# Stick-breaking attention: part of the weight multiplies on GpSimd, with the second sigmoid written to SBUF

## The chip, the cores and the metric

The kernel runs on one core of one Trainium2 chip. The metric is the device time of one execution in microseconds (us), as the median of several runs of the same program. A profile of one execution is used beside it; its span goes from the first to the last instruction.

## The reference

One layer of a transformer block on x of shape (1, 2048, 1024): two kinds of attention side by side, an output projection, and a SwiGLU feed-forward network. The change lies in the stick-breaking attention, which has 8 heads of 64 columns:

```python
def stick_breaking_attention(q, k, v):
    # A[t,s] = beta_ts * prod_{s<j<t}(1 - beta_tj), s < t
    z = einsum('bqhd,bkhd->bhqk', q, k) * 64 ** -0.5
    log_1mb = where(s < t, log_sigmoid(-z), 0.0)
    rem = cumsum(log_1mb, axis=keys, reverse=True) - log_1mb
    a = where(s < t, exp(log_sigmoid(z) + rem), 0.0)
    return einsum('bhqk,bkhd->bqhd', a, v)
```

So for a query t each key s gets beta = sigmoid(z), times the product of (1 - beta) = sigmoid(-z) over all keys between s and t. The other half of the width is differential attention (4 heads, softmax). The outputs of both are normed, joined, multiplied by w_out and added to x; the feed-forward network follows.

## The kernel before

**Stages.** The program has eight head groups. Groups 0 to 3 are differential attention, groups 4 to 7 stick-breaking, two heads each. For each group `proj` multiplies the normed input with 384 columns of w_in (16 row tiles, L320), splits the result into two float16 parts (`split_psum`, L327 or L329 for the high part and L330 for the low one), and transposes q and k by DMA. The projection of the next group is emitted between the attention units of this one (`advance`), and in the last group the output projection (L761) is emitted in its place. The feed-forward network comes behind and holds the second half of the span.

**A unit of stick-breaking.** `stage_a(i, m, b)` takes 128 queries (row tile i), one head m and a block b of up to 1024 keys, in chunks c of up to 512 keys, the last chunk first. There are 192 units with 320 chunks, 224 of them full. For each chunk:

- TensorE writes the scores into a PSUM tile `sc` (L448; four such buffers).
- ScalarE writes sigmoid(-z) into the SBUF tile `om` (L554) and then sigmoid(z) over the scores in `sc` (L555).
- VectorE scans `om` from its end to its start, which leaves the running product in it (L557). The instruction names `sc` as its second operand, which the operation `bypass` doesn't use.
- VectorE multiplies beta from `sc` with the scan shifted by one key, into the SBUF tile `be` (L558). It is the last to read `sc`.

After the chunks, `split_t` splits `be` into two float16 parts in a buffer `s16` (three of them): ScalarE casts the high part (L89), GpSimd subtracts it for the low part (L98). A DMA transpose on SP's queue (L403) brings both into a tile `aT` (five). `stage_b` multiplies `aT` with the values on TensorE (L458), up to five units behind `stage_a`. `be` and `om` come from one pool of nine tiles `z4`; the profile shows both as z.

**What sets the order.** Each engine works off its instructions in order. A scheduler of the framework sets that order when the program is built; it times the instructions by its own model. Which engine gets a piece of work is settled earlier, in the Python code. `note(e, ns)` books planned time to ScalarE, VectorE or GpSimd. `pick(...)` gives the next piece to the engine whose booked load plus cost is least, and books it. `level()` sets all loads to zero, at every fourth row tile of a head group. `split_psum` and `tt` use `pick` too, so what is booked at one place changes the choice at others. Before the change, a chunk booked 3.15 w + 350 to VectorE, w being its keys, and its multiply had no choice.

Of the kernel before, what the change touches and what calls it, by code (L numbers as in the profile page):

```python
# [15 lines left out]
AF = mybir.ActivationFunctionType  # L16
ALU = mybir.AluOpType
# [4 lines left out]
S, D, P = 2048, 1024, 128  # L22
# [37 lines left out]
def block(tc, a, out):  # L60
    nc = tc.nc
    PE, ACT, DVE, POOL, SP = nc.tensor, nc.scalar, nc.vector, nc.gpsimd, nc.sync
    top = ExitStack()
    with top:
# [8 lines left out]
        def note(e, ns):  # L73
            load[e] += ns * KW[e]

        def pick(**cost):
            e = min(cost, key=lambda k: load[k] + cost[k] * KW[k])
            load[e] += cost[e] * KW[e]
            return e

        def level():
            for k in load:
                load[k] = 0.0
# [16 lines left out]
        def pri(k):  # L100
            def deco(f):
                @functools.wraps(f)
                def g(*args):
                    with tc.high_priority(PRI[k]) if PRI[k] else nullcontext():
                        return f(*args)
                return g
            return deco

        def nm(s):
            uid[0] += 1  # L110
            return f"{s}{uid[0]}"
# [139 lines left out]
        with ExitStack() as ph1:  # L251
# [6 lines left out]
            def z4():  # L258
                return zp.tile([P, 1028], F32, tag="z4", bufs=ZB, name=nm("z4"))
# [137 lines left out]
            @pri("spl")  # L397
            def split_t(src, n, he="ADP", le="DP"):
                s16 = s16p.tile([P, 2048], F16, tag="s16", bufs=SB, name=nm("s16"))
                to16(s16[:, :n], src, n, he)  # L400
                tt(s16[:, n : 2 * n], src, s16[:, :n], ALU.subtract, n, le)
                aT = sp.tile([P, 16, P], F16, tag="aT", bufs=AB, name=nm("aT"))
                SP.dma_start_transpose(aT[:, : 2 * n // P, :], s16[:, : 2 * n])  # L403
                return aT
# [36 lines left out]
            def fq(g, i):  # L441
                k = 2 if g == NG - 1 else 4
                return (i % k, k)

            @pri("sc")
            def score_chunk(G, sc, i, q, m, w, cut=False):
                for o in range(2):
                    PE.matmul(sc[:, : 128 * w].rearrange("p (t n) -> p t n", n=P), lhsT=G["q"][i // 4][:, 2 - 2 * o + m, i % 4, :], rhs=G["k"][q][:, m, 0:w, :], start=o == 0, stop=o == 1)  # L448
                if cut:
                    PE.matmul(sc[:, 128 * w - P : 128 * w], lhsT=idb[:], rhs=tri[:], start=False, stop=True, skip_group_check=True)  # L450

            @pri("pv")
            def pv(G, yp, y0, aT, b, n, o, wd, start, stop):
                nb = n // P
                for j in range(nb):
                    v = G["v"][2 * b + j // 4][:, j % 4, :]
                    for q, (a_, v_) in enumerate(((j, o), (j, o + wd), (nb + j, o))):
                        PE.matmul(yp[:, y0 : y0 + wd], lhsT=aT[:, a_, :], rhs=v[:, v_ : v_ + wd], start=start and j == 0 and q == 0, stop=stop and j == nb - 1 and q == 2, skip_group_check=True)  # L458
# [77 lines left out]
            def sb_attn(g, G):  # L536
                last = {}

                @pri("at")
                def stage_a(i, m, b):  # L540
                    L = (i + 1) * 128
                    n = min(1024, L - 1024 * b)
                    be, om = z4(), z4()
                    if b == i // 8:
                        DVE.memset(om[:, n : n + 1], 8192.0)
                    else:
                        DVE.tensor_copy(om[:, n : n + 1], last[m][:, 0:1])
                    last[m] = om
                    for c in range((n - 1) // 512, -1, -1):
                        lo, hi = 512 * c, min(512 * c + 512, n)  # L550
                        w = hi - lo
                        sc = ps.tile([P, 512], F32, tag="sc", bufs=4, name=nm("sc"))
                        score_chunk(G, sc, i, 2 * b + c, m, w // P, b == i // 8 and hi == n)
                        ACT.activation(om[:, lo:hi], sc[:, :w], AF.Sigmoid, scale=G["nkz"][:])  # L554
                        ACT.activation(sc[:, :w], sc[:, :w], AF.Sigmoid, scale=G["kz"][:])  # L555
                        ov = om[:, lo:hi][:, ::-1]
                        DVE.tensor_tensor_scan(ov, ov, sc[:, :w], om[:, hi : hi + 1], op0=ALU.mult, op1=ALU.bypass)  # L557
                        DVE.tensor_tensor(be[:, lo:hi], sc[:, :w], om[:, lo + 1 : hi + 1], ALU.mult)  # L558
                        note("A", 1.7 * w + 400)
                        note("D", 3.15 * w + 350)  # L560
                    return n, split_t(be[:, :n], n, "A", "P")

                ypd = {}

                def stage_b(i, m, b, n, aT):
                    r, k = fq(g, i)
                    if i // k not in ypd:
                        ypd[i // k] = ps.tile([P, 512], F32, tag="yp", name=nm("yp"))
                    yp = ypd[i // k]
                    pv(G, yp, P * r + 64 * m, aT, b, n, 128 * m, 64, r == 0 and m == 0 and b == i // 8, r == k - 1 and m == 1 and b == 0)  # L570
                    if m == 1 and b == 0 and r == k - 1:
                        finish(g, G, i, k, yp)
                        G["fin"] = i + 1

                pend = []
                done = 0
                for i in range(NT):
                    if i % 4 == 0:
                        level()
                    for b in range(i // 8, -1, -1):  # L580
                        for m in range(2):
                            n, aT = stage_a(i, m, b)
                            pend.append((i, m, b, n, aT))
                            if len(pend) > PD:
                                stage_b(*pend.pop(0))
                            done += n // P + CS
                            yield done / (272 + 48 * CS), (i + 1 if b == 0 and m == 1 else i)
                for u in pend:
                    stage_b(*u)
# [638 lines left out]
```

## Time and profile before

| | us |
|---|---|
| median of 3 runs (lowest to highest) | 2779.86 (2775.68 to 2783.71) |
| span of the profiled execution | 2785.0 |

The profiled execution lies just above the highest of the three runs, within their scatter. Busy time by stage:

| us from the start | stage | PE | VectorE | ScalarE | GpSimd | granted clock |
|---|---|---|---|---|---|---|
| 0 to 616 | projections, differential attention | 541.54 | 506.08 | 356.88 | 393.19 | 0.96 |
| 616 to 1405 | stick-breaking, with projections and then the output projection | 642.97 | 664.99 | 581.59 | 419.79 | 0.94 |
| 1405 to 2100 | rest of the output projection, feed-forward network with its weights' preparation | 631.76 | 504.91 | 301.48 | 410.69 | 0.97 |
| 2100 to 2785 | feed-forward network, second half | 673.61 | 324.86 | 121.81 | 221.56 | 1.00 |

A row's busy time is to be held against the length of its stretch, 616, 789, 695 and 685 us. In three of the four stages PE is the busiest engine; in stick-breaking it is VectorE. PE is TensorE's matmuls, PEld its weight loads, DVE is VectorE, ACT ScalarE, POOL GpSimd, SP the queue that issues the DMAs. An arrow in a row of waits points to who was waited for. L-numbers are lines of the kernel before.

### The profile page before, as it was taken

What the parts mean: (1) busy time and instruction counts of PE and PEld (TensorE: products, weight loads), DVE (VectorE), ACT (ScalarE), POOL (GpSimd) and SP (SyncE); (2) the same over time, 40 slices, a digit from 0 to 9 for tenths busy, and PEclk for the clock granted to TensorE, in tenths of its full rate; (3) what the DMA queues carried; (4) which work ended last, traced back from release to release, by engine and by line L of the source; (5) the groups of instructions that cost most, each with busy time, mean ns of one, the idle gap of its engine ahead of it and who ended that gap; (6) DMA issues with size and microseconds to landing.
All of it is one profiled execution on the core that took longest, in us unless ns stands there. A gap on an engine that the chain in (4) does not pass through costs nothing. (4 is left out here: it accounts for less than half of the span.)

```text
span 2785.0 us, 45469 instructions
## 1 busy us (share of the span) xinstructions
PE 2489.9 (89%) x17084; PEld 1409.0 (51%) x17084; DVE 2000.8 (72%) x3782; ACT 1361.8 (49%) x2543; POOL 1445.2 (52%) x1008
## 2 busy tenths in 40 slices
PE   6998989888878786888889798989999999999998
PEld 4665556555545453557775343444444444444443
DVE  6888879687989989876756877777786644434445
ACT  4665656466878788765644534443442212111121
POOL 2567767665544555546665656565654332322323
PEclk9999999999999897999999999999999999999999
DMA  6788787789999998997796565655658844635534
GB/s 225 199 167 184 147 188 163 164 174 205 198 205 198 192 182 160 190 198 205 197 309 253 184 235 189 221 187 191 240 170 299 327 155 178 227 125 190 211 129 166
DMA packets 649133, 551.91 MB, mean 198 GB/s; under 512 B 506624, under 2 KB 574208, under 8 KB 638672
## 3 DMA queue, kind: packets, MB, share of 16 engines
q1 hardware_dynamic: 647088, 546.92, 71.2%
q8 instruction: 134, 2.20, 0.3%
q0 software_dynamic: 512, 1.36, 0.2%
q10 hardware_dynamic: 1312, 0.72, 0.1%
q14 instruction: 87, 0.71, 0.1%
HBM read 265.27 MB, written 151.52 MB: 150 GB/s over the span
## 5 line engine op out<-in xcount | busy, mean ns | idle before, releaser
L98 POOL TENSOR_TENSOR s<-z,s 128x1024 f16<-128x1024 f32 (+7 forms) x288 | 474.1, 1654 | 334.8 <-ACT s L89 299.3
L320 PE MATMUL pj<-w,xt 128*128 128x384 f16 x3072 | 572.3, 334 | 32.6 <-DVE st L330 11.6
L320 PEld LDWEIGHTS <-xt 128*128 128x128 f16 x3072 | 299.9, 100 | 241.8 <-issue 36.3
L448 PE MATMUL sc<-kT,qT 128*128 128x512 f16 (+3 forms) x1280 | 346.9, 362 | 74.6 <-DVE z L558 34.4
L1034 PE MATMUL pd<-wd,act 128*128 128x512 f16 x1848 | 406.2, 379 | 3.3 <-DVE hs L1040 2.4
L557 DVE TENSOR_TENSOR_SCAN z<-z,sc 128x512 f32<-128x512 f32 (+3 forms) x320 | 355.5, 1112 | 68.6 <-ACT sc L555 65.1
L458 PE MATMUL yp<-v,aT 128*128 128x64 f16 (+1 forms) x4896 | 281.2, 207 | 80.0 <-DMA aT<-s 79.2
L458 PEld LDWEIGHTS <-aT 128*128 128x128 f16 x4896 | 245.2, 102 | 169.4 <-DMA aT<-s 105.1
L936 PEld LDWEIGHTS <-wg 128*128 128x128 f16 x1848 | 183.9, 100 | 264.3 <-issue 58.8
L98 POOL TENSOR_TENSOR hs<-hs,cu 128x512 f32<-128x512 f32 x132 | 170.5, 1297 | 238.2 <-DVE cu L1040 82.6
L936 PEld LDWEIGHTS <-wu 128*128 128x128 f16 x1848 | 181.0, 98 | 222.1 <-issue 9.0
L1034 PEld LDWEIGHTS <-act 128*128 128x128 f16 x1848 | 180.6, 98 | 222.6 <-issue 4.7
L98 POOL TENSOR_TENSOR act<-cg,act 128x512 f16<-128x512 f32 x117 | 160.8, 1385 | 247.7 <-ACT act L992 141.5
L98 POOL TENSOR_TENSOR fst<-fst 128x512 f32<-128x512 f32 x97 | 179.6, 1852 | 167.6 <-DVE wd L215 78.6
L1040 DVE SCALAR_TENSOR_TENSOR hs<-pd,c,hs 128x512 f32<-128x512 f32 x192 | 142.1, 748 | 160.8 <-PE pd L1034 159.1
L89 ACT CAST s<-z 128x384 f16<-128x384 f32 (+7 forms) x216 | 170.1, 788 | 151.5 <-DMA aT<-s 56.4
L554 ACT ACTIVATE z<-sc,c 128x512 f32<-128x512 f32 (+3 forms) x320 | 202.6, 633 | 10.6 <-PE sc L448 6.5
L558 DVE TENSOR_TENSOR z<-sc,z 128x512 f32<-128x512 f32 (+3 forms) x320 | 193.3, 606 | 8.1
L992 ACT CAST act<-cg 128x512 f16<-128x512 f32 x132 | 80.6, 617 | 234.2 <-DVE cg L998 190.9
L555 ACT ACTIVATE sc<-sc,c 128x512 f32<-128x512 f32 (+3 forms) x320 | 194.8, 609 | 0.0
L761 PE MATMUL po<-wo,mt 128*128 128x256 f16 x1536 | 181.3, 276 | 11.0 <-DVE xf L764 6.3
L936 PE MATMUL pm<-X,wg 128*128 128x512 f16 x792 | 179.1, 379 | 1.2 <-ACT bx L1109 1.2
(233 smaller groups left out, 4028.4 us busy)
## 6 DMA issues: line engine op xcount, KB each, us to landing
xt<-xs SPq DMA_DIRECT2D x112, 512.0 KB, 4.4
hs<-hd SPq DMA_DIRECT2D x96, 512.0 KB, 4.3
hd<-hs SPq DMA_DIRECT2D x80, 512.0 KB, 3.2
split<-wg SPq DMA_DIRECT2D x11, 1792.0 KB, 10.5
split<-wu SPq DMA_DIRECT2D x11, 1792.0 KB, 10.3
split<-wd SPq DMA_DIRECT2D x11, 1792.0 KB, 10.4
wg<-split SPq DMA_DIRECT2D x11, 1792.0 KB, 7.3
wd<-split SPq DMA_DIRECT2D x11, 1792.0 KB, 8.4
```

The lines of the kernel that those rows point to most:

```text
L89: ACT.copy(dst, src)
L98: (DVE if e == "D" else POOL).tensor_tensor(dst, a_, b_, op)
L320: PE.matmul(pj[:, :384], lhsT=xv[:, xi, kt, :], rhs=G["w"][:, wi, kt, :], start=n == 0, stop=n == 23)
L448: PE.matmul(sc[:, : 128 * w].rearrange("p (t n) -> p t n", n=P), lhsT=G["q"][i // 4][:, 2 - 2 * o + m, i % 4, :], rhs=G["k"][q][:, m, 0:w, ...
L458: PE.matmul(yp[:, y0 : y0 + wd], lhsT=aT[:, a_, :], rhs=v[:, v_ : v_ + wd], start=start and j == 0 and q == 0, stop=stop and j == nb - 1 a ...
L554: ACT.activation(om[:, lo:hi], sc[:, :w], AF.Sigmoid, scale=G["nkz"][:])
L555: ACT.activation(sc[:, :w], sc[:, :w], AF.Sigmoid, scale=G["kz"][:])
L557: DVE.tensor_tensor_scan(ov, ov, sc[:, :w], om[:, hi : hi + 1], op0=ALU.mult, op1=ALU.bypass)
L558: DVE.tensor_tensor(be[:, lo:hi], sc[:, :w], om[:, lo + 1 : hi + 1], ALU.mult)
L761: PE.matmul(po[:, sl], lhsT=mt[:, kt, P * xi : P * xi + P], rhs=wos[2 * h + n][wi][:, kt, :], start=q == 0, stop=q == 23)
L936: PE.matmul(ps_[:].rearrange("p (t n) -> p t n", n=P), lhsT=wv[:, wo, wi, 128 * kt : 128 * kt + 128], rhs=X[xo][:, :, xi, kt, :], start=st ...
L1034: PE.matmul(po[:], lhsT=act[:, ao, xi, 128 * j : 128 * j + 128], rhs=W["d"][:, wo, wi, :], start=start and u == 0 and q == 0, stop=u == nu ...
```

## The change

For each chunk, `pick` now chooses between VectorE ("D") and GpSimd ("P") for the multiply. On "D" all is as before. On "P" the second sigmoid is written to `be` in SBUF and not to `sc`, and GpSimd multiplies `be` in place with the shifted scan. The fixed booking to VectorE falls to the scan's share.

```diff
-                        ACT.activation(sc[:, :w], sc[:, :w], AF.Sigmoid, scale=G["kz"][:])
+                        e = pick(D=1.04 * w + 155, P=2.4 * w + 100)
+                        beta = sc[:, :w] if e == "D" else be[:, lo:hi]
+                        ACT.activation(beta, sc[:, :w], AF.Sigmoid, scale=G["kz"][:])
                         ov = om[:, lo:hi][:, ::-1]
                         DVE.tensor_tensor_scan(ov, ov, sc[:, :w], om[:, hi : hi + 1], op0=ALU.mult, op1=ALU.bypass)
-                        DVE.tensor_tensor(be[:, lo:hi], sc[:, :w], om[:, lo + 1 : hi + 1], ALU.mult)
+                        (DVE if e == "D" else POOL).tensor_tensor(be[:, lo:hi], beta, om[:, lo + 1 : hi + 1], ALU.mult)
                         note("A", 1.7 * w + 400)
-                        note("D", 3.15 * w + 350)
+                        note("D", 2.08 * w + 200)
```

In the built program 148 of the 320 multiplies stand on GpSimd: 117 of the 224 with 512 keys, and 6, 16 and 9 of the 32 each with 384, 256 and 128. Of the 80 units with 1024 keys, 50 have one chunk on each of the two engines. Other choices move with the bookings. Of the projection copies of stick-breaking groups, 45 of `v` and 19 of `st` go from ScalarE (L327) to VectorE (L329). After the output projection 6 subtractions of 1024 elements and 11 of 512 go from GpSimd to VectorE.

The rows below are the built order at one place in the third stick-breaking group, where full units follow each other. Lines of the changed kernel are two higher behind the diff: the second sigmoid is L557, the scan L559, the multiply L560. The scan is printed as SCALAR_TENSOR_TENSOR. z42533 is `be` and z42534 `om` of one unit, z42539 and z42540 of the next, z42547 and z42548 of the one behind; sc2541 and sc2542 are the two chunks of the second. VectorE before:

```order
L557 SCALAR_TENSOR_TENSOR z42534_14931<-z42534_14931,sc2536_14940 128x512
L558 TENSOR_TENSOR z42533_14930<-sc2536_14940,z42534_14931 128x512
L557 SCALAR_TENSOR_TENSOR z42540_14971<-z42540_14971,sc2541_14973 128x512
L558 TENSOR_TENSOR z42539_14970<-sc2541_14973,z42540_14971 128x512
L545 MEMSET z42548_15048 128x1
L557 SCALAR_TENSOR_TENSOR z42540_14971<-z42540_14971,sc2542_14980 128x512
L558 TENSOR_TENSOR z42539_14970<-sc2542_14980,z42540_14971 128x512
```

VectorE with the change, the same units:

```order
L560 TENSOR_TENSOR z42533_14930<-sc2535_14933,z42534_14931 128x512
L547 COPY z42540_14971<-z42510_14819 128x1
L559 SCALAR_TENSOR_TENSOR z42534_14931<-z42534_14931,sc2536_14940 128x512
L559 SCALAR_TENSOR_TENSOR z42540_14971<-z42540_14971,sc2541_14973 128x512
L560 TENSOR_TENSOR z42539_14970<-sc2541_14973,z42540_14971 128x512
L545 MEMSET z42548_15048 128x1
L559 SCALAR_TENSOR_TENSOR z42540_14971<-z42540_14971,sc2542_14980 128x512
```

Each unit has lost the multiply of its second chunk (those of sc2536 and sc2542 are gone), and the next scan stands in its place. GpSimd before, where s162537 is the float16 buffer of the unit z42533, s162543 that of z42539 and s162551 that of z42547 (the L214 rows scale w_out):

```order
L98 TENSOR_TENSOR s162507_14789<-z42503_14771,s162507_14789 128x896
L98 TENSOR_TENSOR s162513_14836<-z42509_14818,s162513_14836 128x896
L98 TENSOR_TENSOR s162537_14947<-z42533_14930,s162537_14947 128x1024
L98 TENSOR_TENSOR s162543_14987<-z42539_14970,s162543_14987 128x1024
L214 TENSOR_SCALAR wo2523_14903<-z42524_14904,sW2530_14912 128x1024
L214 TENSOR_SCALAR wo2523_14903<-z42525_14905,sW2530_14912 128x1024
L98 TENSOR_TENSOR s162551_15065<-z42547_15047,s162551_15065 128x1024
L98 TENSOR_TENSOR s162557_15112<-z42553_15094,s162557_15112 128x1024
```

GpSimd with the change:

```order
L560 TENSOR_TENSOR z42533_14930<-z42533_14930,z42534_14931 128x512
L98 TENSOR_TENSOR s162513_14836<-z42509_14818,s162513_14836 128x896
L560 TENSOR_TENSOR z42539_14970<-z42539_14970,z42540_14971 128x512
L214 TENSOR_SCALAR wo2523_14903<-z42524_14904,sW2530_14912 128x1024
L214 TENSOR_SCALAR wo2523_14903<-z42525_14905,sW2530_14912 128x1024
L98 TENSOR_TENSOR s162537_14947<-z42533_14930,s162537_14947 128x1024
L560 TENSOR_TENSOR z42547_15047<-z42547_15047,z42548_15048 128x512
L98 TENSOR_TENSOR s162543_14987<-z42539_14970,s162543_14987 128x1024
L98 TENSOR_TENSOR s162551_15065<-z42547_15047,s162551_15065 128x1024
L560 TENSOR_TENSOR z42561_15169<-z42561_15169,z42562_15170 128x512
L98 TENSOR_TENSOR s162557_15112<-z42553_15094,s162557_15112 128x1024
```

A multiply of the next unit (z42547) now stands ahead of the subtraction of the unit before it (s162543 from z42539). ScalarE before, from the first sigmoid of z42540 to that unit's cast:

```order
L554 ACTIVATE z42540_14971<-sc2541_14973,c1912_10728 128x512
L555 ACTIVATE sc2541_14973<-sc2541_14973,c1911_10727 128x512
L554 ACTIVATE z42540_14971<-sc2542_14980,c1912_10728 128x512
L555 ACTIVATE sc2542_14980<-sc2542_14980,c1911_10727 128x512
L184 ACTIVATE wo2523_14903,m02531_14913<-z42525_14905 128x1024
L89 CAST s162537_14947<-z42533_14930 128x1024
L554 ACTIVATE z42548_15048<-sc2549_15050,c1912_10728 128x512
L555 ACTIVATE sc2549_15050<-sc2549_15050,c1911_10727 128x512
L554 ACTIVATE z42548_15048<-sc2550_15058,c1912_10728 128x512
L555 ACTIVATE sc2550_15058<-sc2550_15058,c1911_10727 128x512
L89 CAST s162543_14987<-z42539_14970 128x1024
```

ScalarE with the change, from the sigmoids of the unit behind it to the same cast:

```order
L554 ACTIVATE z42548_15048<-sc2549_15050,c1912_10728 128x512
L557 ACTIVATE sc2549_15050<-sc2549_15050,c1911_10727 128x512
L327 ACTIVATE v2517_14862<-pj2546_15018 128x2x64
L554 ACTIVATE z42548_15048<-sc2550_15058,c1912_10728 128x512
L557 ACTIVATE z42547_15047<-sc2550_15058,c1911_10727 128x512
L89 CAST s162537_14947<-z42533_14930 128x1024
L554 ACTIVATE z42554_15095<-sc2555_15097,c1912_10728 128x512
L557 ACTIVATE sc2555_15097<-sc2555_15097,c1911_10727 128x512
L554 ACTIVATE z42554_15095<-sc2556_15105,c1912_10728 128x512
L557 ACTIVATE sc2556_15105<-sc2556_15105,c1911_10727 128x512
L327 ACTIVATE st2516_14861<-pj2546_15018 128x4x64
L89 CAST s162543_14987<-z42539_14970 128x1024
```

Before, the sigmoids of one more unit (z42548) stood ahead of the cast to s162543; now those of two (z42548 and z42554) do. Over all 192 units a cast stood 1.7 chunks behind the last sigmoid of its unit, and now stands 3.1; the value products on TensorE stood 7.3 chunks behind the last scores of their unit, and now stand 9.3.

## The prediction

> **What bounds the kernel now.** I read the page's header and its row of busy slices first, to find the stage that the change touches.
>
> ```profile
> span 2785.0 us, 45469 instructions
> ...
> PE 2489.9 (89%) x17084; PEld 1409.0 (51%) x17084; DVE 2000.8 (72%) x3782; ACT 1361.8 (49%) x2543; POOL 1445.2 (52%) x1008
> ...
> DVE  6888879687989989876756877777786644434445
> ```
>
> Over the whole span TensorE is the busy engine and VectorE has a quarter to spare. That average misleads: each digit is 70 us, and from the eleventh to the seventeenth (some 700 to 1190 us) VectorE stands at 8 or 9. That is the middle of the stick-breaking stage, 616 to 1405. So next I cut that stage into stretches; columns are busy us (instructions) for PE, weight loads, VectorE, ScalarE and GpSimd, then the granted clock, the DMA share and GB/s.
>
> ```profile
> 616.00:700.00 84.00, 69.74 (x664) 45.43 (x662) 65.99 (x133) 61.46 (x130) 44.19 (x31) 0.98 0.96 198
> 700.00:805.00 105.00, 87.10 (x927) 54.81 (x925) 99.09 (x170) 85.60 (x156) 56.55 (x33) 0.99 1.06 216
> 805.00:840.00 35.00, 29.13 (x291) 18.78 (x292) 24.87 (x55) 24.47 (x55) 14.09 (x13) 0.88 0.89 166
> 840.00:1190.00 350.00, 268.84 (x2826) 167.53 (x2824) 323.83 (x564) 282.26 (x535) 184.46 (x119) 0.91 0.93 184
> 1190.00:1405.00 215.00, 188.15 (x1946) 152.07 (x1945) 151.21 (x250) 127.81 (x221) 120.50 (x82) 0.95 0.82 202
> ```
>
> In 700 to 805 and 840 to 1190 VectorE is busy 99.09 + 323.83 = 422.9 of 455 us, 93%. PE has 355.9 (78%), ScalarE 367.9 (81%), GpSimd 241.0 (53%). From 1190 on the output projection is mixed in and PE leads with 188.15 of 215 (87.5%). The table of waits for 700 to 1190 says who stands still for whom (total us, times, longest):
>
> ```profile
> POOL s L98 <- ACT s L89: 206.0, 100, 5.5
> PEld L458 <- DMA aT<-s: 45.4, 42, 3.7
> PEld L448 <- DVE z L558: 42.2, 37, 2.1
> ...
> ACT s L89 <- DMA aT<-s: 22.8, 21, 3.2
> ...
> ACT s L89 <- POOL s L98: 15.8, 16, 2.4
> ```
>
> PE's score products (L448) wait for L558, the very multiply of the change, since it is the last reader of their PSUM tile. GpSimd's 206 us of waiting is its slack. The timeline inside this stage shows one 1024-key unit at full pace (start, duration, engine, line):
>
> ```profile
> 966.07 1.27 DVE L557 TENSOR_TENSOR_SCAN z<-z,sc 128x512 f32<-128x512 f32 x1
> ...
> 967.18 0.68 ACT L554 ACTIVATE z<-sc,c 128x512 f32<-128x512 f32 x1
> ...
> 968.04 1.27 DVE L557 TENSOR_TENSOR_SCAN z<-z,sc 128x512 f32<-128x512 f32 x1
> ...
> 968.90 0.67 ACT L555 ACTIVATE sc<-sc,c 128x512 f32<-128x512 f32 x1
> 969.35 0.69 DVE L558 TENSOR_TENSOR z<-sc,z 128x512 f32<-128x512 f32 x1
> 969.96 1.27 DVE L557 TENSOR_TENSOR_SCAN z<-z,sc 128x512 f32<-128x512 f32 x1
> ...
> 970.12 1.05 ACT L89 CAST s<-z 128x1024 f16<-128x1024 f32 x1 [0.54 <-issue]
> ...
> 971.07 0.68 ACT L554 ACTIVATE z<-sc,c 128x512 f32<-128x512 f32 x1
> 971.24 2.13 POOL L98 TENSOR_TENSOR s<-z,s 128x1024 f16<-128x1024 f32 x1 [1.76 <-ACT s L89]
> ```
>
> VectorE runs scan, multiply, scan, multiply without a gap: 966.07 to 969.96 is 3.89 us a unit. ScalarE runs from 967.18 to the next unit's first sigmoid at 971.07, also 3.89, but idles from 969.57 (968.90 + 0.67) to 970.12, so it needs about 3.34. GpSimd needs 2.13. **VectorE sets the pace of these 455 us**, with ScalarE 14% behind it.
>
> **The change, part by part.** The durations come from the groups by form (mean ns after the bar):
>
> ```profile
> L98 POOL TENSOR_TENSOR fst<-fst 128x512 f32<-128x512 f32 x97 | 179.6, 1852 | 167.6 <-DVE wd L215 78.6 <-DVE wg L215 61.7 <-DVE wu L215 22.8
> ...
> L554 ACT ACTIVATE z<-sc,c 128x512 f32<-128x512 f32 x224 | 156.4, 698 | 6.3 <-PE sc L448 4.3 <-issue 1.4 <-PE sc L450 0.4
> L558 DVE TENSOR_TENSOR z<-sc,z 128x512 f32<-128x512 f32 x224 | 153.4, 686 | 5.6
> ...
> L555 ACT ACTIVATE sc<-sc,c 128x512 f32<-128x512 f32 x224 | 151.1, 675 | 0.0
> ...
> L327 ACT ACTIVATE v<-pj 128x128 f16<-128x128 f32 x127 | 35.4, 281 | 57.1 <-PE pj L320 56.3 <-PE yp L458 0.5
> ...
> L330 DVE SCALAR_TENSOR_TENSOR st<-pj,st 128x256 f16<-128x256 f32 x64 | 25.8, 405 | 4.0 <-ACT st L327 3.9
> ...
> L327 ACT ACTIVATE st<-pj 128x256 f16<-128x256 f32 x64 | 25.2, 394 | 23.3 <-DVE v L330 21.6 <-issue 1.1 <-DVE m L195 0.6
> ...
> L558 DVE TENSOR_TENSOR z<-sc,z 128x384 f32<-128x384 f32 x32 | 17.7, 553 | 0.9
> ...
> L98 POOL TENSOR_TENSOR z<-z,z 128x512 f32<-128x512 f32 x10 | 12.7, 1274 | 4.3 <-DVE z L98 3.7
> ...
> L558 DVE TENSOR_TENSOR z<-sc,z 128x128 f32<-128x128 f32 x32 | 9.2, 288 | 0.8
> ...
> L98 DVE TENSOR_TENSOR hs<-hs,cu 128x512 f32<-128x512 f32 x12 | 7.9, 679 | 2.9 <-DMA hs<-hd 2.9
> ```
> ```profile
> L329 DVE TENSOR_SCALAR v<-pj x1: 266/266/266, 1146.8 to 1146.8; 128x128 f16<-128x128 f32 x1
> ```
>
> 1. *Multiplies leave VectorE.* In the built order it is not a third: 148 of 320 go to GpSimd (117 of 512 keys, 6 of 384, 16 of 256, 9 of 128), so 117 x 0.686 + 6 x 0.553 + 16 x 0.42 (256 keys, midway between the rows of 384 and 128) + 9 x 0.288 = 92.9 us off VectorE.
>
> 2. *The same multiplies on GpSimd.* No row shows this multiply there. The nearest is the subtraction in place on the same kind of tile, z<-z,z, 1.274 us for 512; the dearest of that size is 1.852 (fst, a strided view). The operands here are plain rows, so I take 1.274: 117 x 1.274 plus 7,552 keys of the smaller sizes at the same rate (18.8) is 168 us. Upper end: 1.852 makes it 244; then GpSimd, with 241.0 + 0.69 x 244 = 409 of the 455 us below, leads, and at the same 87% the stretch takes 470, 15 slower. The lower end is VectorE's own 0.686, 90 us; then VectorE still leads and the sum stays. The GPSIMD Engine Reference of the Trainium skill (3.1, elementwise side by side) puts a two-input operation at about 2.5 cycles an element and gives 4497 ns for 2048 elements; an estimate from that is 1.12 us for 512, some 18 us less in all on GpSimd, and the sum below stays, since GpSimd is not its largest term. The trace's 1.274 is used.
>
> 3. *The second sigmoid writes SBUF.* L554 does that already and costs 0.698 against 0.675 into PSUM: 148 x 0.023 = 3.4 us more on ScalarE at most.
>
> 4. *PSUM tiles come free earlier.* In a moved chunk the scan (which still names the score tile as an operand) is the last reader, not the multiply: PE gets the tile 0.69 us earlier, where it waits 42.2 us today. This is how PE profits, and it is in the sum by VectorE's pace; I don't add it again.
>
> 5. *The other choices move too.* The planner now books less on VectorE and more on GpSimd, so 45 v and 19 st copies of the projections go from ScalarE to VectorE. ScalarE loses 45 x 0.281 + 19 x 0.394 = 20.1 us. VectorE gains 45 x 0.266 (one row) + 19 x at most 0.405 (the st form exists only as L330, which also reads SBUF; at least the 0.266 of half its size; I take 0.405) = 19.7. After 1190 us, 6 differences of 1024 and 11 of 512 go from GpSimd to VectorE (nearest row 0.679 for 512, twice that for 1024): 15.6 us in a stretch where VectorE has 151.21 of 215 busy, so PE's 188.15 covers them. If that cover failed, they would cost 15.6.
>
> 6. *Queues.* ScalarE's cast now stands about three chunks behind its unit's last sigmoid, where it stood 1.7, and GpSimd's next multiply can stand ahead of a ready subtraction. Behind both wait the transpose on SP and the value products L458. SP's instructions in this stage keep their count.
>
> The sum for the 455 us, by shares of rows:
>
> ```profile
> 700.00:805.00 105.00, 31.62 (x50) 0.99 1.06 216
> ...
> 840.00:1190.00 350.00, 101.70 (x168) 0.91 0.93 184
> ```
> ```profile
> 700.00:805.00 105.00, 7.17 (x21) 0.99 1.06 216
> ...
> 840.00:1190.00 350.00, 19.25 (x55) 0.91 0.93 184
> ```
>
> The first pair is L558, 133.3 of its 193.3 us, so 69% of item 1 falls here; the second is L327, 26.4 of 38.8, so 68% of item 5's copies. VectorE: 422.9 - 0.69 x 92.9 + 0.68 x 19.7 = 372. ScalarE: 367.9 - 0.68 x 20.1 + 2.3 = 356. GpSimd: 241.0 + 0.69 x 168 = 357. PE stays at 356. Nobody leads by more than 5%, so VectorE will not keep its 93%. What the busiest engine reaches where the load is shared is in the windows: PE 69.74 of 84 (83%) before 700, 29.13 of 35 (83%) at 805, 87.5% after 1190. I take the upper one, 87%, because the unit at full pace still has a floor well below 3.89 (VectorE 3.28 without one multiply, which fills 969.35 to 969.96, ScalarE 3.36, GpSimd 2.13 + 1.27 = 3.40). 372 / 0.87 = 428: **27 us less** than 455. At 93% it would be 400 (55 less), at 90% 413 (42 less), at 83% 448 (7 less). Outside the 455 us I count nothing. The FFN behind starts earlier by the same amount. The profiled span is 2785.0; the three runs lie at 2775.7 to 2783.7 with median 2779.9, so the 27 are taken from the median, as 0.2% between them is the scatter: 2753.
>
> **The rivals.**
>
> *Balance eats it.* With four engines within 5% each stall of one is a stall of all, and the busiest reaches 82%: 372 / 0.82 = 454, no change, 2779. For it: the 83% stretches above and ACT s <- POOL s, 15.8 us even today. Against: GpSimd's 206 us of slack.
>
> *The transposes.* The wait for aT (45.4 us on the loads) takes over: DMA share is already 1.06 and 0.93, and a faster stage asks for more per us. Then 2780 or a little less. Against it, from SP's own waits in 910 to 1190 and the transposed tile's row:
>
> ```profile
> SPq L403 <- POOL s L98: 97.7, 49, 6.8
> ```
> ```profile
> DMA to landing us min/median/max: 2.3/4.4/8.3
> ```
>
> SP stood 97.7 of 280 us waiting for s, so transposes follow their data; they don't pile up.
>
> *Slower: the ring of three s16 buffers.* A buffer lives through cast 1.05, subtraction 2.13 and landing 4.4 (median above), 7.6 us; with three that allows a unit every 2.5 us, hidden under 3.89. A multiply ahead of the subtraction adds 1.27, and if it stands at the head of GpSimd's queue waiting for its scan, a scan, a multiply and another scan of VectorE's queue (1.27 + 0.69 + 1.27) come on top: 12.1 us, 4.03 a unit. It decides from 11.7 us of life (3 x 3.89). Price: 0.14 of 3.89 over 455 us is 17, so 2797. The 22.8 us of ACT s <- DMA aT speak for it; the later place of the cast, which lets the scan finish first, speaks against it. The same page (4.1, engine selection) gives elementwise multiplies on a tile to VectorE and not to GpSimd, which by it is about twice as slow. The rows agree on the price (1.274 against 0.686); the rule decides the time only if GpSimd's queue is on the path, as in this rival.
>
> *It doesn't do what it says:* it moves 46% of the chunks, as counted in item 1; no chance of its own.
>
> **How the numbers follow.** Forecast 0.58 at 2753, its own range 2725 to 2771 (93% to 83% occupancy, less or more). Balance 0.15, transposes 0.08, slower 0.19. About 0.3% (8 us) is what a measurement of this kernel can tell from no change. Faster: the forecast and a little of the balance case, 0.60; within 0.3%: 0.21; slower: 0.19. The range 2723 to 2794 takes in both ends of the forecast, the no-change cases and most of the slower one; it leaves out the dearer multiply of 1.852 together with the ring (some 5%) and a gain above 57 us.
>
> **What would show it.** Right: stick-breaking's end comes some 25 us earlier; VectorE in its dense stretch falls to about 87%; the L448 <- L558 wait shrinks to a third; GpSimd goes to 75 to 85% there; the multiply on GpSimd is near 1.27 us. Wrong: ACT s waiting for POOL z or for aT by more than 50 us in the stage (balance, or the ring); aT waits of PE growing by as much as the L558 waits shrink (transposes); a multiply of 1.6 us or more beside VectorE's scans.

## The result

| | before | with the change |
|---|---|---|
| median (lowest to highest), us | 2781.78 (2775.68 to 2784.83) | 2763.64 (2761.24 to 2767.67) |
| ratio with 95% interval | | 0.9939 (0.9920 to 0.9957) |
| span of the profiled execution | 2785.0 | 2759.5 |

The change makes the kernel 0.6% faster, 18 us by the medians. 27 were forecast. The time lies inside the range. The profiled executions are 25.5 us apart, more than the medians: the span of before lies at the upper end of its kernel's runs, that of after at the lower end. All ratios here leave out two single executions that took far longer than the rest of their kernel, 3653.75 us of before and 7190.59 of halfT_before, and so does the median of halfT_before.

The page of the changed kernel, with the same three rows as before:

```profile
span 2759.5 us, 45543 instructions
...
PE 2477.1 (90%) x17084; PEld 1402.5 (51%) x17084; DVE 1957.5 (71%) x3716; ACT 1348.9 (49%) x2483; POOL 1569.3 (57%) x1134
...
DVE  6888979788888888877757767777686544444445
```

GpSimd has gone from 1445.2 to 1569.3 us busy, VectorE from 2000.8 to 1957.5. The four slices of VectorE that stood at 9 in the middle of stick-breaking stand at 8. To see where the time went I compare by work and not by the clock: the 320 scans come in the same number in both traces, so the starts of the 1st, 41st, 261st and last scan, and of the first product of the feed-forward network, mark the same places in the work. The times are starts of rows of the scan and of that product:

| piece of work | before, us | after, us | difference |
|---|---|---|---|
| start to 1st scan | 618.2 | 612.3 | -5.9 |
| 1st to 41st scan | 105.0 | 95.3 | -9.7 |
| 41st to 261st scan (dense) | 460.4 | 452.0 | -8.4 |
| 261st to last scan (output projection beside it) | 217.5 | 214.8 | -2.7 |
| last scan to feed-forward | 70.8 | 73.7 | +2.9 |
| feed-forward | 1313.1 | 1311.4 | -1.7 |

The first row is no effect of the change: up to there both programs have the same instructions in the same order. It is the scatter between two executions, and what lies below some 5 us in one row is not to be built on. **The dense stretch, on which the forecast put all of its 27 us, gave 8 by these marks.** But the marks hold only the scans fixed, not what is done beside them. The windows from the 1st to the 41st scan, of before and then of after (length, then PE, weight loads, VectorE, ScalarE, GpSimd, clock, DMA share, GB/s):

```profile
618.20:723.10 104.90, 89.36 (x838) 56.99 (x836) 84.52 (x169) 77.28 (x162) 55.46 (x39) 0.98 0.97 199
```
```profile
612.30:707.60 95.30, 79.08 (x765) 50.73 (x764) 76.86 (x160) 72.60 (x145) 69.88 (x56) 1.00 0.98 197
```

PE's work is 10.3 us less here, and 6.0 us more in the dense windows below: projections have moved over the mark. So of the second and the third row only the sum can be read, 565.4 us before and 547.3 after. **From the 1st to the 261st scan the change saves 18.1 us, as good as its whole gain**; the last three rows add up to 1.5 less. The windows of the dense stretch, before and after:

```profile
723.00:1184.00 461.00, 359.42 (x3792) 224.93 (x3790) 421.06 (x742) 370.54 (x703) 238.77 (x152) 0.92 0.95 189
```
```profile
708.00:1160.00 452.00, 365.46 (x3851) 228.98 (x3850) 383.28 (x698) 359.42 (x657) 339.78 (x252) 0.93 0.99 197
```

VectorE's work fell by 37.8 us there, the stretch by 9. So VectorE went from 91% to 85% busy, and no engine has taken its place: PE 81%, ScalarE 80%, GpSimd 75%. The same windows' waits, before:

```profile
POOL s L98 <- ACT s L89: 190.9, 96, 4.6
PEld L458 <- DMA aT<-s: 42.4, 40, 3.7
...
DVE z L557 <- ACT sc L555: 24.4, 31, 3.2
...
ACT s L89 <- DMA aT<-s: 18.0, 18, 3.2
```

and after:

```profile
POOL s L98 <- ACT s L89: 54.7, 40, 4.5
PEld L458 <- DMA aT<-s: 54.3, 41, 4.6
ACT s L89 <- DMA aT<-s: 50.2, 43, 3.4
POOL z L560 <- DVE z L559: 46.1, 37, 3.6
...
DVE z L559 <- ACT z L557: 26.2, 20, 4.6
DVE z L559 <- ACT sc L557: 24.1, 24, 5.2
```

GpSimd's slack behind the cast has shrunk from 190.9 us to 54.7. ScalarE's cast now waits 50.2 us for a transpose to land, where it waited 18.0, and VectorE's scans wait 50.3 us for ScalarE (26.2 + 24.1), where it was 24.4. How these belong together is seen in the timeline of the changed kernel around 845 us:

```profile
838.31 5.46 SPq L403 DMA_TRANSPOSE aT<-s  x2
...
845.08 1.05 ACT L89 CAST s<-z 128x1024 f16<-128x1024 f32 x1 [3.42 <-DMA aT<-s]
...
846.20 4.22 POOL L98 TENSOR_TENSOR s<-z,s 128x1024 f16<-128x1024 f32 x2 [3.29 <-ACT s L89]
...
847.80 0.36 ACT L557 ACTIVATE z<-sc,c 128x128 f32<-128x128 f32 x1
...
848.20 0.48 DVE L559 TENSOR_TENSOR_SCAN z<-z,sc 128x128 f32<-128x128 f32 x1 [4.61 <-ACT z L557]
```

Two transposes take SP's queue 5.46 us from 838.31 on. ScalarE comes to the next cast, and stands 3.42 us until a landing frees one of the three s16 buffers. That buffer's own cast had begun at 832.19; GpSimd began the subtraction at 834.92, SP issued the transpose at 838.31, and it landed at 844.98, 12.8 us after the cast began. Behind the cast in its queue are the next sigmoids, so VectorE stands 4.61 us before its scan, and GpSimd 3.29. Where nothing of that kind happens, the pace is as it was worked out:

```profile
942.17 1.28 DVE L559 TENSOR_TENSOR_SCAN z<-z,sc 128x512 f32<-128x512 f32 x1
...
942.25 1.89 POOL L98 TENSOR_TENSOR s<-z,s 128x896 f16<-128x896 f32 x1 [0.73 <-ACT s L89]
...
943.37 1.27 DVE L559 TENSOR_TENSOR_SCAN z<-z,sc 128x512 f32<-128x512 f32 x1
...
944.10 1.10 POOL L560 TENSOR_TENSOR z<-z,z 128x512 f32<-128x512 f32 x1
...
945.35 1.28 DVE L559 TENSOR_TENSOR_SCAN z<-z,sc 128x512 f32<-128x512 f32 x1
...
948.66 1.27 DVE L559 TENSOR_TENSOR_SCAN z<-z,sc 128x512 f32<-128x512 f32 x1
```

The second scans of three units start at 942.17, 945.35 and 948.66, 3.2 to 3.3 us apart where before a unit took 3.89. The row of 943.37 is the next unit's first scan, with no multiply ahead of it; the one that stood there is the row of 944.10, on GpSimd.

### The profile page after: what moved, and what is told of

The parts are those of the page before. It is cut to its first block, busy times and chain, and to the rows that moved or that the text cites. A ratio compares the mean times of both kernels' runs of the same rounds, so it can differ in the third digit from the quotient of the medians.

```text
span 2759.5 us, 45543 instructions
## 1 busy us (share of the span) xinstructions
PE 2477.1 (90%) x17084; PEld 1402.5 (51%) x17084; DVE 1957.5 (71%) x3716; ACT 1348.9 (49%) x2483; POOL 1569.3 (57%) x1134
## 5 line engine op out<-in xcount | busy, mean ns | idle before, releaser
L559 DVE TENSOR_TENSOR_SCAN z<-z,sc 128x512 f32<-128x512 f32 (+3 forms) x320 | 353.2, 1113 | 82.4 <-ACT sc L557 40.4
L448 PE MATMUL sc<-kT,qT 128*128 128x512 f16 (+3 forms) x1280 | 341.1, 359 | 48.8 <-DVE z L559 17.1
L938 PEld LDWEIGHTS <-wu 128*128 128x128 f16 x1848 | 181.5, 98 | 222.3 <-issue 10.3
L560 POOL TENSOR_TENSOR z<-z,z 128x512 f32<-128x512 f32 (+3 forms) x148 | 152.5, 1033 | 96.8 <-DVE z L559 79.7
L938 PE MATMUL pm<-X,wu 128*128 128x512 f16 x792 | 178.3, 379 | 0.0
## 6 DMA issues: line engine op xcount, KB each, us to landing
split<-wg SPq DMA_DIRECT2D x11, 1792.0 KB, 10.5
split<-wu SPq DMA_DIRECT2D x11, 1792.0 KB, 10.3
split<-wd SPq DMA_DIRECT2D x11, 1792.0 KB, 10.5
```

Of the source, the lines that this page charges most:

```text
L560: (DVE if e == "D" else POOL).tensor_tensor(be[:, lo:hi], beta, om[:, lo + 1 : hi + 1], ALU.mult)
L938: PE.matmul(ps_[:].rearrange("p (t n) -> p t n", n=P), lhsT=wv[:, wo, wi, 128 * kt : 128 * kt + 128], rhs=X[xo][:, :, xi, kt, :], start=st ...
```

## The experiments

All ratios are to the kernel before on the same chip, with 95% intervals. Each kernel is built and ordered anew by the scheduler, so besides its edit each has an order of its own.

### What carries the gain

**book**: the change's bookings, all multiplies on VectorE.

```diff
-                        beta = sc[:, :w] if e == "D" else be[:, lo:hi]
+                        beta = sc[:, :w]
-                        (DVE if e == "D" else POOL).tensor_tensor(...)
+                        DVE.tensor_tensor(...)
```

> The bookings of the change stay (so 64 projection copies move from ScalarE to VectorE), but every multiply stays on VectorE and reads the score tile as before. VectorE pace theory: VectorE gets 20 us more work and loses none, so the time is that of before or worse, 2782 to 2800. Rival (the gain comes from the shifted copies and the new order, not from the multiplies): near the changed kernel, 2764 to 2770.

Measured: 2779.12 us, 0.9988 (0.9978 to 0.9999). As good as no change. The gain isn't the shifted copies. Nor do the 20 us that they add to VectorE show in full: its dense stretch takes 464.3 us, 4 more than before, where VectorE's share alone would say 13.

**sbuf**: the second sigmoid in SBUF for the 148 chunks, multiplied in place by VectorE.

```diff
-                        (DVE if e == "D" else POOL).tensor_tensor(...)
+                        DVE.tensor_tensor(...)
```

> As the changed kernel, with the second sigmoid of the same 148 chunks in SBUF, but VectorE does all multiplies in place; GpSimd gets none. VectorE pace theory: no relief of VectorE, 2780 to 2800. Rival (the score tile that comes free at the scan is what pays): 2764 to 2772, though VectorE is as busy as before.

Measured: 2813.99 us, 1.0116 (1.0097 to 1.0136), slower than either theory had it. Here the PSUM tile comes free at the scan as in the change, and it saves nothing that shows; but the test isn't clean, since the multiply got dearer. The line's rows (min, median, max ns):

```profile
L560 DVE TENSOR_TENSOR z<-sc,z x172: 275/679/693, 616.9 to 1428.5; 128x512 f32<-128x512 f32 x107, 128x384 f32<-128x384 f32 x26, 128x128 f32<-128x128 f32 x23, 128x256 f32<-128x256 f32 x16
L560 DVE TENSOR_TENSOR z<-z,z x148: 264/692/2614, 627.3 to 1423.2; 128x512 f32<-128x512 f32 x117, 128x256 f32<-128x256 f32 x16, 128x128 f32<-128x128 f32 x9, 128x384 f32<-128x384 f32 x6
```
```profile
L560 DVE TENSOR_TENSOR z<-z,z 128x512 f32<-128x512 f32 x117 | 106.9, 914 | 1.7
...
L560 DVE TENSOR_TENSOR z<-sc,z 128x512 f32<-128x512 f32 x107 | 73.3, 685 | 3.2 <-DVE z L559 0.5
```

From the score tile a multiply of 512 takes 0.685 us and never more than 0.693. With both operands in SBUF it takes 0.914 on average and up to 2.614. That is 117 x 0.229 = 27 us more work for VectorE, beside the copies that it gets here as in book, and the time rises by 32. From the 1st to the 261st scan VectorE's work rises from 505.2 to 549.4 us and the stretch from 565.4 to 603.0. What the tile that comes free earlier is worth by itself stays open.

**moveonly**: the same 148 chunks on GpSimd (PAT lists them), with the bookings of before.

```diff
-                        e = pick(D=1.04 * w + 155, P=2.4 * w + 100)
+                        e = PAT[turn[0]]
+                        turn[0] += 1
...
-                        note("D", 2.08 * w + 200)
+                        note("D", 3.15 * w + 350)
```

> The same 148 chunks multiply on GpSimd, but the bookings are those of before, so the 64 projection copies stay on ScalarE. VectorE pace theory: VectorE saves another 13 us in the dense stretch, so some 5 to 12 us faster than the changed kernel, 2752 to 2759. Rival (ScalarE and its wait for a free s16 buffer pace the stage now): ScalarE has 20 us more, so no faster or slower than the changed kernel, 2764 to 2778.

Measured: 2767.81 us, 0.9949 (0.9934 to 0.9964). The moved multiplies alone carry the gain, within what can be told. Taking another 20 us of copies off VectorE brings nothing: in the dense stretch its work is 374.6 us where the change has 383.3, and ScalarE's, with the copies, 372.4 where it has 359.4, but the stretch takes 459.1 us. So in the changed kernel VectorE's load no longer sets the time by itself. The expectation of the VectorE theory was missed; the time lies in the range of the other.

### How many, and which chunks

In these four the choice is by a fixed rule, and each choice is booked at the change's costs:

```diff
-                        e = pick(D=1.04 * w + 155, P=2.4 * w + 100)
+                        e = "P" if turn[0] % 3 == 2 else "D"            # third
+                        e = "D" if turn[0] % 3 == 2 else "P"            # twothirds
+                        e = "P" if n > 512 and c == 1 else "D"          # firstc
+                        e = "P" if n > 512 and c == 0 else "D"          # secondc
+                        note(e, 1.04 * w + 155 if e == "D" else 2.4 * w + 100)
```

> Every third chunk is GpSimd's, 106 of 320. VectorE pace theory: the gain goes with the number moved, 106/148 of 18 us, so 2768 to 2770. Queue theory: fewer moved multiplies wait, so as good as the changed kernel or better, 2758 to 2766.

> Two of three chunks are GpSimd's, 214 of 320. GpSimd then has more work than VectorE in the dense stretch (241 + 0.69 x 240 = 407 of 455 us at 1.13 us a multiply). VectorE pace theory with GpSimd's own load left out: 26 us gain, 2756. GpSimd as the bound: 2775 to 2800.

> GpSimd multiplies the first chunk in each of the 128 units of two chunks (80 of them full), and no other. VectorE loses about 75 us of multiplies. Queue theory (a multiply that waits for its scan at the head of GpSimd's queue, and the cast that waits for it, eat the relief): the first chunk's multiply is ready while VectorE still works on the second, so GpSimd's wait for the scan falls well below the 79.7 us of the changed kernel and the time is 5 to 15 us better, 2749 to 2759. VectorE pace theory: less is moved than in the changed kernel, so 2764 to 2770.

> GpSimd multiplies the second chunk in the same 128 units, all of 512 keys, and no other. VectorE loses 88 us. VectorE pace theory: about as the changed kernel and some us better than with the first chunks, 2760 to 2766. Queue theory: the cast of each such unit waits for GpSimd, so 5 us or more slower than with the first chunks, 2764 to 2778.

| chunks on GpSimd | median, us | ratio | dense stretch, us | 1st to 261st scan, us |
|---|---|---|---|---|
| 0 (before) | 2781.91 | 1 | 460.4 | 565.4 |
| 106, third | 2766.22 | 0.9944 (0.9932 to 0.9956) | 453.2 | 552.2 |
| 128, firstc | 2770.43 | 0.9955 (0.9942 to 0.9968) | 452.9 | 553.2 |
| 128, secondc | 2768.39 | 0.9949 (0.9931 to 0.9966) | 451.9 | 552.1 |
| 148, the change | 2763.64 | 0.9939 (0.9920 to 0.9957) | 452.0 | 547.3 |
| 148, moveonly | 2767.81 | 0.9949 (0.9934 to 0.9964) | 459.1 | 553.4 |
| 214, twothirds | 2790.22 | 1.0031 (1.0019 to 1.0043) | 474.9 | 563.1 |

From 106 to 148 the time doesn't depend on the number by what can be told, and the dense stretch ends at 452 to 459 us whatever is moved: something else holds it there. At 214 the time lies where it was expected with GpSimd as the bound, but GpSimd isn't full: it is busy 379.4 of the 474.9 us, 80%, and ScalarE's wait for a landing has grown to 80.2 us. First or second chunk makes no difference that can be told, though the cast stands 2.4 chunks behind its unit's last sigmoid in the one order and 3.7 in the other. The queue theory, that the cast's wait for GpSimd's multiply eats the relief, gets no support, but these two runs don't test it well: GpSimd's wait for the scan, which the first chunk was to shorten, is 75.4 us in the dense stretch of firstc, 29.3 in that of secondc and 46.1 in the changed kernel.

### The ring of s16 buffers

A fourth buffer has room only if the y tile of `finish` has one buffer in place of two.

```diff
-QB, KB, ZB, AB, SB, PD = 4, 7, 9, 5, 3, 5
+QB, KB, ZB, AB, SB, PD = 4, 7, 9, 5, 4, 5                                      # sb4_after, sb4_before
-                y = sp.tile([P, 512], F32, tag="y", bufs=2, name=nm("y"))
+                y = sp.tile([P, 512], F32, tag="y", bufs=1, name=nm("y"))      # and y1_after
```

> The changed kernel with four s16 buffers in place of three (and one y buffer in place of two, to make room). Ring theory: ScalarE's wait for aT's transposes (82.4 us in the stage) falls below 30 us and the time by 8 to 20 us, to 2744 to 2756. VectorE pace theory (VectorE is still what sets the time): within 4 us of the changed kernel, 2760 to 2768.

> The changed kernel with one y buffer in place of two and three s16 buffers as before: what the room for the fourth s16 buffer costs by itself. If the single y buffer is what made four s16 buffers slower than the changed kernel (2775.7 against 2763.6): 2772 to 2785, and the fourth buffer is worth something. If it costs nothing: 2762 to 2767, and the fourth buffer itself is of no use.

> The kernel before with four s16 buffers and one y buffer. VectorE pace theory: the ring is not the limit there, so 2778 to 2788 (the y buffer's cost included). If the ring were the limit already: below 2774.

| | median, us | ratio | dense stretch, us | 1st to 261st scan | 261st to last scan |
|---|---|---|---|---|---|
| sb4_after | 2775.74 | 0.9977 (0.9966 to 0.9988) | 454.5 | 552.7 | 216.1 |
| y1_after | 2780.78 | 0.9991 (0.9980 to 1.0001) | 461.6 | 559.3 | 222.5 |
| sb4_before | 2773.39 | 0.9966 (0.9952 to 0.9980) | 460.0 | 563.4 | 205.4 |

sb4_after lies outside the ranges of both theories, because the single y buffer costs the changed kernel its whole gain. Against y1_after the fourth s16 buffer wins back 5 us by the medians (the intervals overlap). The waits of sb4_after in its dense stretch, 720 to 1172:

```profile
PEld L458 <- DMA aT<-s: 65.5, 58, 6.0
POOL z L560 <- DVE z L559: 57.0, 38, 9.2
...
ACT s L89 <- DMA aT<-s: 23.2, 13, 3.6
```

ScalarE's wait for the landing halves, from 50.2 to 23.2, and part of what it lost stands at PE's wait for aT, 65.5 after 54.3. More buffers shift some of the wait from the cast to the value products. In the kernel before, the fourth buffer changes nothing in the dense stretch, as expected there, but the stretch with the output projection is 12 us shorter and the kernel 0.34% faster, below its expectation. How much of that is the buffer's own isn't known: book and sbuf, with three buffers, take 209.9 and 208.9 us in that last stretch.

### Half the transposes

**halfT_after, halfT_before**: in stick-breaking, transpose the high half of s16 alone; the low half's product with the values takes the high half once more.

```diff
-                SP.dma_start_transpose(aT[:, : 2 * n // P, :], s16[:, : 2 * n])
+                if he == "A":
+                    SP.dma_start_transpose(aT[:, : n // P, :], s16[:, :n])
+                else:
+                    SP.dma_start_transpose(aT[:, : 2 * n // P, :], s16[:, : 2 * n])
...
-                    for q, (a_, v_) in enumerate(((j, o), (j, o + wd), (nb + j, o))):
+                    for q, (a_, v_) in enumerate(((j, o), (j, o + wd), ((j if wd == 64 else nb + j), o))):
```

> The same cut of the transposes in the kernel before. VectorE pace theory: VectorE sets the time there, so 0 to 6 us, 2776 to 2782. If the transposes set it there too: 10 us or more, below 2772.

> The changed kernel, but in stick-breaking only the high half of s16 is transposed, so each transpose moves half; the low half's product with the values takes the high half again. TensorE, GpSimd, ScalarE and VectorE do the same work. Transposes theory (what is left is set by the landing of aT, which PE and ScalarE wait for): 10 to 30 us faster than the changed kernel, 2734 to 2754. Balance theory (four engines near each other in load, and each one's queue stalls the next): less than 8 us, 2756 to 2766.

| | median, us | ratio | dense stretch, us | 1st to 261st scan | 261st to last scan |
|---|---|---|---|---|---|
| halfT_before | 2756.78 | 0.9914 (0.9899 to 0.9928) | 458.8 | 557.9 | 193.9 |
| halfT_after | 2721.74 | 0.9786 (0.9771 to 0.9800) | 422.6 | 523.1 | 203.1 |

Before the change, the edit leaves the dense stretch about where it was, 458.8 after 460.4 us, and takes 7.5 us off the way from the 1st to the 261st scan: VectorE sets most of the time there. With the change, it takes the dense stretch from 452.0 to 422.6 and that way from 547.3 to 523.1. In all the changed kernel gains 42 us, more than the 10 to 30 that were expected. The windows and waits of halfT_after in the dense stretch:

```profile
716.00:1138.00 422.00, 351.19 (x3797) 223.62 (x3797) 378.28 (x690) 355.01 (x652) 332.36 (x250) 0.94 0.70 148
```
```profile
PEld L461 <- DMA aT<-s: 44.2, 34, 3.5
...
ACT s L89 <- DMA aT<-s: 4.1, 4, 2.3
```

VectorE is at 378.28 of 422, 90% busy, with PE at 83%, ScalarE at 84% and GpSimd at 79%, so loads near each other don't by themselves keep it at 85%. ScalarE's wait for a landing is 4.1 us where it was 50.2. The median time from issue to landing of these transposes, from the DMA issues of the same windows, is 4.4 us in the changed kernel and here 3.2:

```profile
aT<-s SPq DMA_TRANSPOSE x133, 4.4
```
```profile
aT<-s SPq DMA_TRANSPOSE x130, 3.2
```

**The edit takes away more than bytes.** The high half is written by ScalarE's cast alone, so the transpose no longer waits for GpSimd's subtraction. SP's own waits show it, in the changed kernel and then in halfT_after:

```profile
SPq L403 <- POOL s L98: 108.6, 62, 4.8
SPq L403 <- POOL z L560: 73.1, 45, 4.3
```
```profile
SPq L404 <- ACT sc L560: 80.4, 38, 8.4
SPq L404 <- ACT s L89: 42.6, 23, 5.6
```

Casts, subtractions and transposes of the dense stretch, paired in the order in which they run (131 or 132 units of all sizes), give these means:

| us | cast | to the subtraction's start | subtraction | to SP's issue | issue to landing | from the cast's start to the landing |
|---|---|---|---|---|---|---|
| before | 0.81 | 0.26 | 1.61 | 0.90 | 4.54 | 8.11 |
| the change | 0.82 | 1.03 | 1.64 | 0.98 | 4.56 | 9.02 |
| halfT_before | 0.81 | | | 0.43 behind the cast | 3.41 | 4.65 |
| halfT_after | 0.84 | | | 0.81 behind the cast | 3.49 | 5.14 |

Of the 3.9 us between the change and halfT_after, 1.1 are the shorter transfer; the rest is the subtraction that is no longer waited for. So the two runs show that the way from the cast to aT holds the changed kernel back, and the kernel before much less. They don't show which part of it does. From before to the change the transfer took no longer, and what grew most is the wait for GpSimd's subtraction, by 0.77 us. A kernel that halves the bytes and still waits for the subtraction wasn't run.

The total of halfT_before missed its expectation (2757, where 2776 to 2782 stood), mainly in the last stretch, which went from 217.5 to 193.9 us; PE's work between those marks fell from 189.1 to 174.9, so part of that is work done elsewhere. In the total the edit brings 0.9% before the change and 1.5% with it.

## Why the prediction was right, and where it wasn't

The sign and the range held, and so did the first half of the mechanism: VectorE bounded these stretches, and multiplies taken off it shorten them. The gain is 18 us and not 27, because behind VectorE stood something for which the sum had no term of its own.

- *What bounds the kernel before.* VectorE sets the pace of the dense stretch: shown, by halfT_before and sb4_before, which leave that stretch at 459 and 460 us, and by sbuf, where VectorE's work in it rises from 421 to 456 us and the stretch to 497.
- *Item 1, multiplies off VectorE.* 64 us were counted for the dense stretch. In the windows of the dense stretch VectorE's multiplies fell from 133.3 us to 71.3, by 62. Right.
- *Item 2, their price on GpSimd.*

```profile
L560 POOL TENSOR_TENSOR z<-z,z 128x512 f32<-128x512 f32 x117 | 132.6, 1134 | 86.1 <-DVE z L559 71.0 <-DVE xrs L150 4.4 <-DVE z L545 3.8
...
L329 DVE TENSOR_SCALAR v<-pj 128x128 f16<-128x128 f32 x46 | 12.6, 277 | 2.8 <-PE pj L320 2.4 <-PE yp L458 0.4
...
L329 DVE TENSOR_SCALAR st<-pj 128x256 f16<-128x256 f32 x19 | 7.9, 415 | 0.0
```

1.134 us for 512, less than the 1.274 of the row that was taken. All 148 take 152.5 us, not 168. The estimate from the GPSIMD Engine Reference of the Trainium skill (3.1), 1.12 us, was the better one. Nothing hung on the difference.

- *Item 5, the copies.* VectorE's v and st copies cost 0.277 and 0.415 us (0.266 and 0.405 were taken). The windows' 37.8 us less for VectorE, where 50.7 were counted over about the same work, have 15.3 of copies in them where 13.4 were counted; the rest, 9 us, is of other lines, mainly two more pieces of w_out's scaling (4.9) and three more projected tiles (2.3) that lie in the stretch now. book and moveonly show no difference in time by the copies that can be told.
- *Item 6, the queues.* It named the late cast and the multiply ahead of a ready subtraction, and no term of the sum stands for either. The cast's place made no difference between firstc and secondc that can be told. The subtraction does start later, 1.03 us behind its cast where it was 0.26.
- *The step that failed is the occupancy.* 372 us of VectorE's work were divided by 0.87, the share of the busiest engine in stretches with another mix. Measured are 383 us of work at 85%. From the 1st to the 261st scan VectorE is busy 460.1 of 547.3 us, 84%; at 87% that work would have taken 529. PE at 81% and ScalarE at 80% make that look like the balance rival, but the runs show a place: **the way from the cast to the landing of aT**. With that way cut from 9.0 to 5.1 us the same work runs at 90%. Of the 38 us by which the change with the shorter way shortens the dense stretch of before (460.4 to 422.6), the full way holds back 29.
- *The transposes* had a chance of 0.08. The argument against them was that SP waits for its data 97.7 us of 280, so that they don't pile up. That held: in the changed kernel SP waits for GpSimd 181.7 us of 452, and a transfer takes 4.56 us on average where it took 4.54. Yet ScalarE's wait for a landing nearly tripled in the dense stretch.
- *The ring rival* named the right place, the s16 buffer whose life ends at the landing, and a cause that the trace shows, the subtraction that starts later. It had the effect too large: the life grew from 8.1 to 9.0 us and not to 12.1, and it took part of the gain and didn't turn it over. Its sign came out: in the stage ScalarE waits 82.4 us for aT, more than the 50 that the prediction named, where it waited 37.3 before. A fourth buffer, with a y buffer given up for it, doesn't mend it. Whether the wait for the subtraction, the time of one transpose or the load of the 16 DMA engines (share 0.99, and 0.70 with half the bytes) counts most stays open: the edit changes all three.
- *Nothing outside the dense stretch.* This can't be judged by the rows. The work from the 1st to the 41st scan took 105.0 us before, 99.0 with 106 multiplies moved, 95.3 with the change and 88.3 with 214, but PE's work between these marks fell with it, from 89.5 to 84.5, 79.1 and 75.3 us, so that PE was 83 to 85% busy in all four. What grew shorter is mostly what lay between the marks.
- *The chances.* Faster by over 0.3% had 0.60 and came out. That the time came out well inside the forecast's own range of 2725 to 2771 is in part luck, since its working had too high a share and no price for the way to aT.

The two ratios of the kernels with half the transposes, 0.9786 over 0.9914, make the change worth 1.3% there, about twice the 0.6% that it brings with whole ones. No version within the reference's computation beat the changed kernel by what can be told; third, with 106 multiplies moved, equals it.

## What to carry to other kernels

An engine at 93% in a stretch is worth relieving, but divide the relieved work by an occupancy only after asking which ring of buffers sits a few per cent behind: here three buffers, each in use for 8.1 of the 10.5 us in which three units pass, came to 9.0 of 10.3 as the pace went up and the subtraction ahead of their transfer came to wait for other work. A test that shortens the suspected way in both kernels, with all arithmetic left in place, tells the old bound from the new one in two runs; look then at what else the edit took away, here a wait for another engine. Marks in the work are good for comparing only if the work between them is the same on every engine. And if one stretch ends at nearly the same length for every amount moved, stop moving work and look for what holds it.

## What the runs showed of the hardware

- VectorE's multiply of 512 float32 took 0.685 us with one operand in PSUM, at most 0.693 beside any work of GpSimd, but 0.914 on average and up to 2.614 with both in SBUF (run sbuf). Of the 117 rows of 512 with both in SBUF, the 53 that started while a GpSimd tensor operation was under way average 1.19 us, the other 64 average 0.68 and take at most 0.694. The Trainium skill's page SBUF — State Buffer (who interferes with whom) says that a VectorE instruction with two SBUF inputs contends with a GpSimd instruction that reads SBUF, and that one with at most one SBUF input, outside the 2-port modes, doesn't; both halves agree with these rows.
- GpSimd's in-place multiply of 512 took 1.134 us on average in the changed kernel, where its in-place subtraction z<-z,z of the same size took 1.274 in the kernel before.
